# Moving the first four prompt-memory loads from SyncE's DMA queue to ScalarE's in a one-core decoder step

## The chip, the core and the metric

The kernel runs on one core of a Trainium2 chip. The core has TensorE (PE; its weight loads are listed apart as PEld), VectorE (DVE), ScalarE (ACT), GpSimd (POOL) and SyncE (SP). SP and ACT can each issue DMA transfers from their own instruction stream; the profile marks an issue as SPq or ACTq. The metric is the device time of one execution in microseconds.

## The reference

The program computes one layer of a decoder for 256 prompt tokens and 32 sample tokens together (T = 288 columns), in float32, with model width 2048. Cut to what matters here:

```
mk, mv = memory_kv(mem_prompt)          # rms_norm(mem) @ w_mem_kv, 256 memory tokens
h = rms_norm(x) * g_mix
proj = h @ w_in                         # conv, stick-breaking attention, memory query, gates
y_conv, y_sb, y_mem = three branches
x = x + (gates * branches summed) @ w_o
x = x + relu(rms_norm(x) @ w_up)^2 @ w_down
```

The first matrix product on the chip is the one for the prompt memory, `rms_norm(mem_prompt) @ w_mem_kv`: 256 memory tokens by 2048 features, into 512 value and 512 key columns. It is the only part that the change touches.

## The kernel before

All weights lie in DRAM as 504 slabs of 128 x 1024 float32 (512 KB), in the order in which they are used. A slab is loaded into a tile `wr`. Since TensorE is to give float32 accuracy, each slab is split: ScalarE rounds it to a high part `wh` (line 303), VectorE subtracts that from `wr` and leaves a low part `wl` (line 314). Activations are split the same way, and each product is three matmuls: high by high, low by high, high by low. There are four buffers of `wr` and four pairs of `wh` and `wl`.

The first 16 slabs hold the memory projection, two for each pair of feature blocks: one with value columns ("v"), one with key columns ("k"). These slabs are loaded in two halves of 256 KB. Beside them the raw prompt memory comes in eight tiles named `s` (128 x 512 float32), each in two halves of 128 KB (`memT`, line 394). A half is one feature block of 128 features by 256 memory tokens. For each half, ScalarE (line 345; for the very first half VectorE, line 341) multiplies by the gain and rounds to a high part `a`, VectorE makes the low part (line 361), and ScalarE squares the tile for the norm (lines 350 and 352).

On TensorE, `warm_up` runs seven matmuls on a constant tile (line 1419), then `mem_products` runs 32 turns of six 128x512 matmuls each (line 539). A turn takes one feature block and either the value or the key columns. The first four turns are (block 0, v), (block 0, k), (block 1, v), (block 1, k): they need both halves of the first two slabs and of the first `s` tile.

The order of instructions on every engine is fixed when the program is built. Each piece of work is a Python generator that asks for an engine, a time and the events it needs; a planner (`Order.run`) simulates the engines with fixed costs and emits the instructions in the order in which the simulation starts them. `add(gen, rank)` puts a generator in, and the lower rank goes first when two could start together. `loads` issues all loads on SP. `sp(...)` asks for 0.45 us of SP, and `order.landed(kb)` is the planner's guess of when a transfer lands.

Every DMA raises one of eight completion semaphores, `DMAHW0` to `DMAHW7`, taken in rotation over all DMAs of both queues in emission order. A DMA that takes a semaphore a second time first waits until its earlier user has landed; this wait stands in the instruction stream of the engine that issues the DMA.

Of the kernel before, what the change touches and what calls it, by code (L numbers as in the profile page):

```python
# [14 lines left out]
P = 128  # L15
# [59 lines left out]
class Order:  # L75
# [15 lines left out]
    def add(self, gen, rank, at=None):  # L91
        job = Job(gen, rank, self.now.ready if at is None and self.now else at or 0.0)
        self.jobs.append(job)
        was, self.now = self.now, job
        self.step(job)
        self.now = was
# [10 lines left out]
    def give(self, pool, n=1):  # L107
        self.pools[pool] += [self.now.ready] * n
# [45 lines left out]
def dve(n, *flags, **take):  # L154
    return Ask("DVE", 0.18 + n / 920.0, flags, **take)


def act(n, *flags, **take):
    return Ask("ACT", 0.22 + n / 1200.0, flags, **take)
# [10 lines left out]
def sp(*flags, **take):  # L170
    return Ask("SP", 0.45, flags, **take)
# [11 lines left out]
def tile_decoder_step(ctx: ExitStack, tc: tile.TileContext, xT, memT, wall, cvec, kmat, ptab,  # L183
                      kpool, vpool, mkc, mvc, hist,
                      yT, oK, oV, oCp, oCs, oMK, oMV):
    nc = tc.nc
# [15 lines left out]
    order = Order(bufs)  # L202
    give, add, done = order.give, order.add, order.set
# [3 lines left out]
    def tl(p, shape, dt=F32):  # L207
        cnt[0] += 1
        return pools[p].tile(shape, dt, tag=p, name=f"{p}_{cnt[0]}")
# [46 lines left out]
    def col(c):  # L256
        return cv[:, c:c + 1]
# [18 lines left out]
    def load_slab(s, part):  # L276
        sl = slabs[s]
        if part == 0:
            sl.raw = tl("wr", [P, SLAB])
        n = SLAB // sl.parts  # L280
        nc.sync.dma_start(sl.raw[:, part * n:(part + 1) * n], wall[s, :, part * n:(part + 1) * n])
        sl.landed[part].at = order.landed(n * P * 4 / 1e3)
# [5 lines left out]
    def due(s):  # L288
        return at_slab[1] + 2.9 * (s - at_slab[0])
# [3 lines left out]
    def cast_weights():  # L293
        todo = [(0, 0), (1, 0), (0, 1), (1, 1)] + [(s, i) for s in range(2, N_SLABS) for i in range(slabs[s].parts)]
        for s, i in todo:
            sl = slabs[s]
            n = SLAB // sl.parts
            cast_at[0] = s
            yield act(n, sl.landed[i], **({} if i else {"w": 1}))
            if i == 0:  # L300
                sl.h = shifted("wh", s)
            c = slice(i * n, (i + 1) * n)
            nc.scalar.copy(sl.h[:, c], sl.raw[:, c])  # L303
            sl.split[i].cast = order.now.ready
            add(sub_part(s, i), lambda s=s: 0 if due(s) - order.free["DVE"] < 5.0 else 4.5)
# [30 lines left out]
    def prep_mem(k2, raw, here):  # L336
        for i in range(2):
            if k2 + i == 0:
                yield dve(ML, here[i], a=2)
                a = hm[0] = Acts(ML)  # L340
                nc.vector.tensor_scalar_mul(a.h, raw[:, i], col(C_GMEM))
            else:
                yield act(ML, here[i], a=2)
                a = hm[2 * k2 + i] = Acts(ML)
                nc.scalar.mul(a.h, raw[:, i], col(C_GMEM + 2 * k2 + i))
            add(prep_low(a, raw[:, i], C_GMEM + 2 * k2 + i, ML, hm_in[2 * k2 + i]), 0.5 + 0.01 * k2)
        yield act(2 * ML, hm_in[2 * k2 + 1])
        if k2 == 0:
            mem_sum.append(tl("s", [P, 512]))
            nc.scalar.activation(mem_sum[0], raw.rearrange("p k t -> p (k t)"), AF.Square)  # L350
        else:
            nc.scalar.activation(raw, raw, AF.Square)
            yield dve(2 * ML)
            nc.vector.tensor_add(mem_sum[0], mem_sum[0], raw.rearrange("p k t -> p (k t)"))
            give("s")
            if k2 == KT // 2 - 1:
                done(sums_m)

    def prep_low(a, raw, c, n, flag):
        yield dve(n, late=Order.HOP)  # L360
        nc.vector.scalar_tensor_tensor(a.l, raw, col(c), a.h.bitcast(F32), op0=ALU.mult, op1=ALU.subtract)
        done(flag)

    def prep_x(k, raw, here, last):
        yield act(T, here, a=2)
        a = hx[k] = Acts()
        nc.scalar.mul(a.h, raw, col(C_GMIX + k))
        add(prep_low(a, raw, C_GMIX + k, T, hx_in[k]), 1.5 + 0.01 * k)
        yield act(T, hx_in[k], **({"t": 1} if k == 0 else {}))
        if k == 0:  # L370
            x_sum.append(tl("t", [P, T]))
            nc.scalar.activation(x_sum[0], raw, AF.Square)
        else:
            nc.scalar.activation(raw, raw, AF.Square)
            yield dve(T)
            nc.vector.tensor_add(x_sum[0], x_sum[0], raw)
        if last:
            give("k4")
        if k == KT - 1:
            done(sums_x)  # L380

    def loads():

        xs = [(0, 3), (3, 6), (6, 9), (9, 12), (12, 15), (15, 16)]
        for k2 in range(KT // 2):
            yield sp(s=1)
            raw = tl("s", [P, 512]).rearrange("p (k t) -> p k t", k=2)
            here = [Flag(), Flag()]
            for i in range(2):
                for what in ("vmk" if k2 + i == 0 else "mvk"):  # L390
                    if what == "m":
                        if k2 + i:
                            yield sp()
                        nc.sync.dma_start(raw[:, i], memT[:, 2 * k2 + i, :])
                        here[i].at = order.landed(131)
                        if i == 0:
                            add(prep_mem(k2, raw, here), 0.5 + 0.01 * k2)
                    else:
                        yield sp(**({} if i else {"wr": 1}))
                        load_slab(2 * k2 + "vk".index(what), i)  # L400
            if k2 >= 1 and xs:
                k0, k1 = xs.pop(0)
                yield sp(k4=1)
                x = tl("k4", [P, 1024])[:, :(k1 - k0) * T].rearrange("p (k t) -> p k t", k=k1 - k0)
                nc.sync.dma_start(x, xT[:, k0:k1, :])
                there = Flag()
                there.at = order.landed(147 * (k1 - k0))
                for k in range(k0, k1):
                    add(prep_x(k, x[:, k - k0], there, k == k1 - 1), 1.5 + 0.01 * k)
            if k2 == 1:  # L410
                yield sp()
                nc.sync.dma_start(cv[:, C_BGATE:], cvec[:, C_BGATE:])
            if k2 == 2:
                yield sp()
                nc.sync.dma_start(km, kmat)
                km_in.at = order.landed(213)
                yield sp()
                nc.sync.dma_start(pt, ptab)
                pt_in.at = order.landed(1) + 20.0
        for s in range(KT, N_SLABS):  # L420
            yield sp(wr=1)
            load_slab(s, 0)
# [39 lines left out]
    def mem_norm():  # L462
        yield dve(ML, sums_m)
        both = mem_sum[0][:, :ML]
        nc.vector.tensor_add(both, both, mem_sum[0][:, ML:])
        yield act(ML, t=2)
        h, l = tl("t", [P, T], F32R)[:, :ML], tl("t", [P, T], F32R)[:, :ML]
        nc.scalar.copy(h, both)
        yield dve(ML)
        nc.vector.tensor_sub(l, both, h.bitcast(F32))  # L470
        give("s")
        yield pe(0.45, pa=1)
        ss = bank("pa")[:, :2 * MT].rearrange("p (m c) -> p m c", c=2)
        for m in range(MT):
            for x in (h, l):
                nc.tensor.matmul(ss[:, m], x[:, m * P:(m + 1) * P], ones_r[:, 0:2], start=x is h, stop=x is l)
        give("t", 2)
        ss = ss[:, :, 0]
        yield from rsqrt_of(ss, MT, D_MODEL, nm[0][:, :MT], nm[1][:, :MT], rm)
        give("pa")  # L480
        done(rm_done)
# [510 lines left out]
    def read_pages():  # L992

        for i in range(2 * NB):
            yield Ask("SP", 0.6, (pt_in,), 2.5)
            pages.append(nc.sync.value_load(pt[0:1, i:i + 1], min_val=0, max_val=kpool.shape[0] - 1))
        done(pages_in)
# [457 lines left out]
                yield from main_tile(u, down_tile(j, c == D_FF // D_MODEL - 1))  # L1455

    with tc.manual_schedule():
        add(loads(), 1.0)
        add(cast_weights(), lambda: 0 if due(cast_at[0]) - order.free["ACT"] < 6.0 else 4.5)
        add(mem_norm(), 0.6)  # L1460
        add(sum_norm(x_sum, D_MODEL, rx, rx_done, sums_x), 0.6)
        add(main(), 20.0)
        add(conv_norm(), 8.0)
        add(read_pages(), 4.0)
        add(make_homes(), 1.0)
        order.run()
# [156 lines left out]
```

## Time and profile before

| what | value |
|---|---|
| median of three runs | 1629.76 us (1629.35 to 1629.9) |
| the profiled execution, its own time | 1629.18 us |
| span of the profiled execution, first to last instruction | 1627.2 us |
| PE busy, share of the span | 1622.6 us, 100% |
| DVE, ACT, POOL busy | 994.0, 736.9, 139.0 us |
| bytes moved by DMA | 305.33 MB, mean 188 GB/s |
| granted TensorE clock, mean | 1.000 |

The span starts with the first instruction; the time of the execution is 1.98 us longer than the span. Times in the timeline count from the start of the span. Matmuls are pipelined, so the duration of a matmul row is longer than the distance from one matmul to the next; distances are read from the starts. In the timeline a row with "x2" is two like instructions merged, with the start of the first and the stretch of both.

### The profile page before, as it was taken

The numbers are of one execution on the slowest core, as the hardware profiler recorded it, in microseconds if no ns is written. First come the engines' busy times: TensorE is split into PE (matmuls) and PEld (weight loads), VectorE is DVE, ScalarE is ACT, GpSimd is POOL, SyncE is SP. The second block draws the span as 40 slices with busy tenths as digits, with TensorE's granted clock in tenths as the row PEclk, the third lists the DMA queues.
The fourth block names the chain that finished last, engine by engine and source line by source line (L and its number), as shares of the span: only waits on it lengthen the run. The fifth ranks groups of instructions, "written<-read, shape, count | busy, mean of one in ns | idle before, by whom it ended". The sixth has DMA issues, their size and how long they took to land.

```text
span 1627.2 us, 30882 instructions
## 1 busy us (share of the span) xinstructions
PE 1622.6 (100%) x12744; PEld 1606.7 (99%) x12744; DVE 994.0 (61%) x1478; ACT 736.9 (45%) x1082; POOL 139.0 (9%) x106
## 2 busy tenths in 40 slices
PE   9999999999999999999999999999999999999999
PEld 7999999999999999999999999999999999999999
DVE  8899888877777655565555544455445554455543
ACT  8746766654434534444443333333333333333332
POOL 0020000000000000001222200121001210022100
PEclk9999999999999999999999999999999999999999
DMA  9787476677755555556655555555555555555663
GB/s 336 217 176 263 141 270 198 208 260 265 243 167 171 170 170 172 166 164 206 194 173 169 170 171 168 169 169 169 168 168 169 169 169 168 170 169 169 180 192 101
DMA packets 107103, 305.33 MB, mean 188 GB/s; under 512 B 19922, under 2 KB 29522, under 8 KB 106962
## 3 DMA queue, kind: packets, MB, share of 16 engines
q1 hardware_dynamic: 106818, 303.33, 60.1%
q8 instruction: 100, 1.64, 0.4%
q14 instruction: 41, 0.34, 0.1%
q10 hardware_dynamic: 144, 0.02, 0.0%
HBM read 296.99 MB, written 6.32 MB: 186 GB/s over the span
## 4 chain that ended last, share of the span: by engine, by line
PE 100%; POOL 0%; DVE 0%; issue 0%; POOLq 0%
PE pm L486 93%; PE pm L539 3%; PE pa L486 1%; PE pl L1021 1%; PE pl L1195 0%; PE pa L860 0%; PE pa L862 0%; PE pa L861 0%; PE pl L1035 0%; PE pa L1419 0%; PE pa L1157 0%; PE pa L825 0%; PE pa L915 0%; PE pa L1171 0%; PE pa L1129 0%; PE pa L1112 0%
## 5 line engine op out<-in xcount | busy, mean ns | idle before, releaser
L303 ACT CAST wh<-wr 128x1024 fp32r<-128x1024 f32 (+1 forms) x520 | 530.4, 1023 | 638.3 <-PE pm L486 581.8
L486 PE MATMUL pm<-a,wh 128*128 128x288 f32 x5184 | 737.1, 293 | 0.0
L314 DVE TENSOR_TENSOR wl<-wr,wh 128x1024 fp32r<-128x1024 f32 (+1 forms) x520 | 620.1, 1196 | 190.7 <-ACT wh L303 188.5
L486 PEld LDWEIGHTS pm<-a,wh 128*128 128x128 f32 x5184 | 696.2, 188 | 0.0
L486 PE MATMUL pm<-a,wl 128*128 128x288 f32 x2592 | 399.2, 293 | 0.0
L486 PEld LDWEIGHTS pm<-a,wl 128*128 128x128 f32 x2592 | 359.0, 188 | 0.6 <-issue 0.6
L486 PE MATMUL pm<-k,wh 128*128 128x288 f32 x2400 | 337.8, 292 | 0.0
L486 PEld LDWEIGHTS pm<-k,wh 128*128 128x128 f32 x2400 | 321.5, 188 | 0.0
L486 PE MATMUL pm<-k,wl 128*128 128x288 f32 x1200 | 181.8, 292 | 0.0
L486 PEld LDWEIGHTS pm<-k,wl 128*128 128x128 f32 x1200 | 165.5, 188 | 0.0
L1356 POOL TENSOR_TENSOR t<-t 128x288 f32<-128x288 f32 x64 | 96.7, 1511 | 599.5 <-DVE t L1353 599.5
L1370 DVE TENSOR_TENSOR a<-a,pm 128x288 f32<-128x288 f32 x64 | 29.1, 455 | 122.3 <-PE pm L486 122.3
L1353 DVE SCALAR_TENSOR_TENSOR t<-pm,rx 128x288 f32<-128x288 f32 x64 | 29.3, 458 | 90.2 <-PE pm L486 90.2
L1359 ACT CAST k<-t 128x288 fp32r<-128x288 f32 x60 | 25.9, 433 | 124.1 <-POOL t L1356 124.1
L1272 DVE TENSOR_TENSOR t<-pm,rx 128x288 f32<-128x288 f32 x48 | 22.0, 458 | 70.9 <-PE pm L486 70.9
L1361 DVE TENSOR_TENSOR k<-t,k 128x288 fp32r<-128x288 f32 x60 | 27.4, 459 | 59.3 <-ACT k L1359 59.3
L717 DVE SCALAR_TENSOR_TENSOR a<-a,cv,a 128x256 f32<-128x256 f32 x120 | 59.5, 496 | 1.3
L1342 POOL TENSOR_TENSOR t<-t,t 128x288 f32<-128x288 f32 x15 | 21.2, 1415 | 418.0 <-ACT t L1339 418.0
L539 PE MATMUL pm<-wh,a 128*128 128x512 f32 x128 | 35.0, 395 | 0.0
L486 PE MATMUL pm<-s,wh 128*128 128x288 f32 x160 | 33.7, 292 | 0.0
L539 PEld LDWEIGHTS pm<-wh,a 128*128 128x128 f32 x128 | 24.2, 190 | 5.9 <-ACT wh L303 1.0
L486 PEld LDWEIGHTS pm<-s,wh 128*128 128x128 f32 x160 | 25.6, 188 | 0.0
(211 smaller groups left out, 744.3 us busy)
## 6 DMA issues: line engine op xcount, KB each, us to landing
wr<-in_wall SPq DMA_DIRECT2D x488, 512.0 KB, 3.7
wr<-in_wall SPq DMA_DIRECT2D x32, 256.0 KB, 4.8
k<-in_kpool SPq DMA_DIRECT2D x32, 256.0 KB, 5.8
k<-in_vpool SPq DMA_DIRECT2D x32, 256.0 KB, 6.2
k<-in_mkc SPq DMA_DIRECT2D x8, 512.0 KB, 9.0
k<-in_mvc SPq DMA_DIRECT2D x8, 512.0 KB, 7.3
t<-in_xT SPq DMA_DIRECT2D x16, 144.0 KB, 3.8
out_yT<-a SPq DMA_DIRECT2D x16, 144.0 KB, 1.9
```

The costliest lines, as they stand in the source:

```text
L303: nc.scalar.copy(sl.h[:, c], sl.raw[:, c])
L314: nc.vector.tensor_sub(sl.l[:, c], sl.raw[:, c], sl.h[:, c].bitcast(F32))
L486: nc.tensor.matmul(ps, w, a, start=(first and i == 0), stop=(last and i == len(todo) - 1))
L539: nc.tensor.matmul(ps[m], y[:, m * P:(m + 1) * P], z[:, w], start=(k == 0 and j < 2), stop=(k == KT - 1 and j in (4, 5)))
L717: nc.vector.scalar_tensor_tensor(c[:, :NP], up[:, k:k + NP], w, c[:, :NP], op0=ALU.mult, op1=ALU.add)
L1272: nc.vector.tensor_mul(g, ps, rx)
L1342: nc.gpsimd.tensor_add(sq_sum[0], sq_sum[0], res[0])
L1353: nc.vector.scalar_tensor_tensor(r, ps, 0.0, r2, op0=ALU.max, op1=ALU.mult)
L1356: nc.gpsimd.tensor_mul(r, r, r)
L1359: nc.scalar.copy(a.h, r)
L1361: nc.vector.tensor_sub(a.l, r, a.h.bitcast(F32))
L1370: nc.vector.tensor_add(x1[j], x1[j], ps)
```

## The change

A new generator `lead` issues both halves of the first two `s` tiles (four transfers of 128 KB) from ScalarE's instruction stream. `loads` then leaves the memory out for the first two pairs of feature blocks and issues only the weight halves there, in the order v, k, v, k. Everything after that is issued on SP as before.

```diff
+    LEAD = 2
+
+    def lead():
+
+        for k2 in range(LEAD):
+            for i in range(2):
+                yield Ask("ACT", 0.45, **({} if i else {"s": 1}))
+                if i == 0:
+                    raw = tl("s", [P, 512]).rearrange("p (k t) -> p k t", k=2)
+                    here = [Flag(), Flag()]
+                    add(prep_mem(k2, raw, here), 0.5 + 0.01 * k2)
+                nc.scalar.dma_start(raw[:, i], memT[:, 2 * k2 + i, :])
+                here[i].at = order.landed(131)
+
     def loads():
...
         for k2 in range(KT // 2):
-            yield sp(s=1)
-            raw = tl("s", [P, 512]).rearrange("p (k t) -> p k t", k=2)
-            here = [Flag(), Flag()]
+            if k2 >= LEAD:
+                yield sp(s=1)
+                raw = tl("s", [P, 512]).rearrange("p (k t) -> p k t", k=2)
+                here = [Flag(), Flag()]
             for i in range(2):
-                for what in ("vmk" if k2 + i == 0 else "mvk"):
+                for what in ("vk" if k2 < LEAD else "mvk"):
                     if what == "m":
-                        if k2 + i:
-                            yield sp()
+                        yield sp()
                         nc.sync.dma_start(raw[:, i], memT[:, 2 * k2 + i, :])
...
     with tc.manual_schedule():
+        add(lead(), 0.0)
         add(loads(), 1.0)
```

Since the planner sees other times, it numbers the tiles otherwise and changes the order in a few places later in the program too.

On SP, at the start of the program, the order before was as follows. `wr_126` is the first value slab, `wr_129` the first key slab, `wr_136` and `wr_140` the next pair; `s_117` and `s_134` are the first two memory tiles. A row names the semaphore that the issue waits for.

```order
L281 DMA wr_126<-in_wall 128x512
L394 DMA s_117<-in_memT 128x256
L281 DMA wr_129<-in_wall 128x512
L394 DMA s_117<-in_memT 128x256
L281 DMA wr_126<-in_wall 128x512
L281 DMA wr_129<-in_wall 128x512
L394 DMA s_134<-in_memT 128x256
L281 DMA wr_136<-in_wall 128x512 [waits DMAHW0_49]
L281 DMA wr_140<-in_wall 128x512 [waits DMAHW1_49]
L394 DMA s_134<-in_memT 128x256 [waits DMAHW2_49]
```

On SP with the change, the same place (`wr_119` is now the first value slab, `wr_130` the first key slab, `wr_137` and `wr_139` the next pair):

```order
L281 DMA wr_119<-in_wall 128x512
L281 DMA wr_130<-in_wall 128x512
L281 DMA wr_119<-in_wall 128x512
L281 DMA wr_130<-in_wall 128x512
L281 DMA wr_137<-in_wall 128x512 [waits DMAHW0_49]
L281 DMA wr_139<-in_wall 128x512 [waits DMAHW2_49]
L281 DMA wr_137<-in_wall 128x512 [waits DMAHW3_49]
L281 DMA wr_139<-in_wall 128x512 [waits DMAHW4_49]
```

The four memory transfers are gone from SP: the first half of the key slab stands second instead of third, and the eight weight halves follow each other.

On ACT, at the start of the program, before (`wh_138` and `wh_153` are the high parts of the first value and key slab; `cv` is a table of gains):

```order
L228 ACT_TABLE_LOAD
L240 DMA cv<-in_cvec 128x48
L303 CAST wh_138<-wr_126 128x512 [waits DMAHW0_49]
L303 CAST wh_153<-wr_129 128x512 [waits DMAHW3_49]
L345 ACTIVATE a_157<-s_117,cv 128x256 [waits DMAHW4_49,DMAHW2_49]
L303 CAST wh_138<-wr_126 128x512 [waits DMAHW5_49]
L303 CAST wh_153<-wr_129 128x512 [waits DMAHW6_49]
```

On ACT with the change (`wh_149` and `wh_163` are now those high parts, `s_132` is the second memory tile; "x2" is two like rows in a row):

```order
L228 ACT_TABLE_LOAD
L240 DMA cv<-in_cvec 128x48
L393 DMA s_117<-in_memT 128x256 x2
L393 DMA s_132<-in_memT 128x256
L393 DMA s_132<-in_memT 128x256 [waits DMAHW1_49]
L303 CAST wh_149<-wr_119 128x512 [waits DMAHW0_49]
L345 ACTIVATE a_157<-s_117,cv 128x256 [waits DMAHW5_49,DMAHW2_49]
L303 CAST wh_163<-wr_130 128x512
L345 ACTIVATE a_166<-s_132,cv 128x256 [waits DMAHW7_49]
L303 CAST wh_149<-wr_119 128x512 [waits DMAHW3_49]
```

All four memory issues now stand ahead of ScalarE's first cast, and the last of them is the ninth DMA of the program, so it waits for a semaphore, `DMAHW1`. Who raises that semaphore is told by VectorE's rows with the change, where the subtraction that reads the first half of the key slab `wr_130` waits for it:

```order
L361 SCALAR_TENSOR_TENSOR a_143<-s_117,cv,a_142 128x256 [waits DVE_49]
L314 TENSOR_TENSOR wl_160<-wr_119,wh_149 128x512 [waits DMAHW0_49,Activation_49]
L361 SCALAR_TENSOR_TENSOR a_158<-s_117,cv,a_157 128x256 [waits DMAHW5_49,Activation_49]
L314 TENSOR_TENSOR wl_169<-wr_130,wh_163 128x512 [waits DMAHW1_49,Activation_49]
L361 SCALAR_TENSOR_TENSOR a_167<-s_132,cv,a_166 128x256 [waits DMAHW7_49,Activation_49]
```

What moved: the cast of the first key half had a wait of its own before; now it has none, because an instruction further up on its engine, the issue of the second half of `s_132`, has waited for the same transfer.

## The prediction

> **What bounds the kernel now.** I read the page first, for the bound, then the waits of the weight loads, then a table by stage, then the timeline of the first 12 us, where the change lies.
>
> ```profile
> span 1627.2 us, 30882 instructions
> PE 1622.6 (100%) x12744; PEld 1606.7 (99%) x12744; DVE 994.0 (61%) x1478; ACT 736.9 (45%) x1082; POOL 139.0 (9%) x106
> ...
> PE 100%; POOL 0%; DVE 0%; issue 0%; POOLq 0%
> ```
>
> The chain that ended last (the third line) is TensorE's own work from end to end. So only two things can move the time: TensorE's amount of work, which the change leaves as it is, and idle or slow stretches on TensorE. The waits of the weight loads, in order of their total (us in total, times, longest), show how few there are:
>
> ```profile
> PEld pa L1419 <- POOL eps L233: 1.3, 1, 1.3
> PEld pm L539 <- ACT wh L303: 1.0, 2, 0.6
> PEld pm L486 <- issue: 0.6, 2, 0.4
> PEld pm L539 <- DVE wl L314: 0.4, 1, 0.4
> ```
>
> The first is the start of the program. The second and fourth are in the memory stage: 1.4 us in which TensorE's loads waited for a split weight. All other waits together are small. The table by stage (stretch, its length, then busy time and count of PE, PEld, DVE, ACT, POOL, the clock, the DMA share, GB/s):
>
> ```profile
> 0.00:10.00 10.00, 8.68 (x25) 6.05 (x26) 4.40 (x9) 5.63 (x10) 1.24 (x8) 1.00 0.78 248
> 10.00:50.00 40.00, 40.00 (x180) 33.22 (x179) 37.50 (x68) 36.61 (x75) 0.25 (x2) 1.00 0.98 333
> 50.00:540.00 490.00, 490.00 (x4207) 483.73 (x4206) 399.73 (x731) 273.13 (x501) 19.59 (x17) 1.00 0.68 214
> ```
>
> Only the first 10 us have room. From 10 us on PE is busy all the time, though between 10 and 50 us ACT and DVE are over 90% busy and the DMA engines 98%. Now the first 12 us, cut to the rows that matter (start, length, engine, line, what):
>
> ```profile
> 0.75 0.40 SPq L281 DMA_DIRECT2D wr<-in_wall  x1
> 0.77 0.40 ACTq L240 DMA_DIRECT2D cv<-in_cvec  x1
> 1.21 0.42 SPq L394 DMA_DIRECT2D s<-in_memT  x1
> ...
> 1.32 3.35 PE L1419 MATMUL pa<-wh 128*128 128x512 f32 x7 [1.32 <-POOL eps L233]
> 1.67 0.44 SPq L281 DMA_DIRECT2D wr<-in_wall  x1
> ...
> 3.76 0.62 ACT L303 CAST wh<-wr 128x512 fp32r<-128x512 f32 x1 [1.74 <-DMA wr<-in_wall]
> ...
> 4.11 0.35 DVE L341 TENSOR_SCALAR a<-s,cv 128x256 fp32r<-128x256 f32 x1 [2.17 <-DMA s<-in_memT]
> 4.41 0.69 DVE L314 TENSOR_TENSOR wl<-wr,wh 128x512 fp32r<-128x512 f32 x1
> ...
> 4.61 1.19 PE L539 MATMUL pm<-wh,a 128*128 128x512 f32 x2
> ...
> 5.18 0.76 PEld L539 LDWEIGHTS pm<-wl,a 128*128 128x128 f32 x2
> 5.60 0.90 PE L539 MATMUL pm<-wl,a 128*128 128x512 f32 x2
> ...
> 6.21 0.80 SPq L281 DMA_DIRECT2D wr<-in_wall  x2
> 6.21 0.62 ACT L303 CAST wh<-wr 128x512 fp32r<-128x512 f32 x1 [1.84 <-DMA wr<-in_wall]
> ...
> 6.34 1.28 PE L539 MATMUL pm<-wh,a 128*128 128x512 f32 x4
> ...
> 8.19 1.53 PE L539 MATMUL pm<-wh,a 128*128 128x512 f32 x6
> ...
> 9.33 0.41 PEld L539 LDWEIGHTS pm<-wl,a 128*128 128x128 f32 x2
> 9.46 0.98 ACT L345 ACTIVATE a<-s,cv 128x256 fp32r<-128x256 f32 x2
> 9.56 0.62 PE L539 MATMUL pm<-wl,a 128*128 128x512 f32 x2
> ...
> 10.01 1.07 PE L539 MATMUL pm<-wh,a 128*128 128x512 f32 x4
> ...
> 10.60 1.66 ACT L303 CAST wh<-wr 128x512 fp32r<-128x512 f32 x3 [0.15 <-DMA wr<-in_wall]
> ...
> 11.37 1.07 PE L539 MATMUL pm<-wh,a 128*128 128x512 f32 x4
> ```
>
> The first cast starts at 3.76, when the first value half has landed; the first real matmul follows at 4.61. The second cast, of the first key half (issued third, at 1.67), waits until 6.21; SP's issue at 6.21 waits for the same transfer. So that half took 6.21 - 1.67 = 4.54 us.
>
> I measure TensorE's start by one number. At full rate a turn of six matmuls takes 11.37 - 10.01 = 1.36 us, 0.227 each, and from 8.19 on the starts keep that step (8.19 + 6 x 0.227 = 9.55, the next row). At 8.19 ten matmuls are done; had they run at full rate without waits, the first would have started at 8.19 - 2.27 = 5.92. This **even start** of 5.92, against the real 4.61, holds all that is lost at the beginning: 1.3 us. Part of that is slow matmuls: the seven of the warm-up took 3.35 us, 0.48 each, and the first two real ones stand (5.60 - 4.61)/2 = 0.50 apart, a small wait included. After that the chain has 192 matmuls in one piece, to 49.61, followed by PE alone:
>
> ```profile
> 4.67 44.94 PE pm L539 x192
> ```
>
> So the end of the program moves by what the even start moves. This bounds the gain too: even with no wait and no slow matmul, the even start can't come before 4.61 with the first cast where it is, so at most 1.3 us can be won. About 0.2% is what a measurement of this kernel can tell from no change, 3.26 us.
>
> **The change part by part.** SP loses four issues of 0.42 to 0.43 us. Its first weight half stays where it is, at 0.75; the first key half goes from 1.67 to about 1.2, the others from 2.63 and 3.1 to 1.7 and 2.1. The ninth DMA and those after it wait for a free semaphore, before and after, so SP stands still from about 2.5 until the first value half has landed (3.76): of the 1.7 us that SP wins, little comes through.
>
> ACT gains four issues of about 0.40 us each (the row at 0.77). Three of them, from 1.17 to about 2.4, cost nothing: ACT waited 1.74 us there for the first weight. The first memory half is issued at 1.2 as before, so VectorE's first product (4.11) isn't later by itself. The fourth issue is the costly one. It waits for the first key half, and it stands ahead of the first cast. So the first cast, which before waited for the first value half alone, now also waits for the first key half, and then for 0.40 us of issue. Behind it queue all of ACT's casts, behind these DVE's subtractions, and behind both TensorE.
>
> How late is that? Call L the landing of the first key half. No row shows two loaded queues at once, so I bound it by the durations of weight halves in the first 20 us, from issue to landing:
>
> ```profile
> DMA to landing us min/median/max: 3.0/4.7/5.3
> ```
>
> Issued at 1.2, it lands between 4.2 and 6.5; by its own 4.54 at 5.75, by the median at 5.9. I take 5.8. The 3.0 belongs to the very first transfer, which had the DMA engines to itself, so it is the far end. The bytes say the same: before, 664 KB of issued data (256 + 128 + 24 + 256) had to move until this half was in; now 512 KB of weights, 24 KB of gains and whatever of the other queue's memory halves comes between, up to 256 KB, so 536 to 792 KB. The transfer rate in half microseconds (last column, GB/s) shows why it took so long:
>
> ```profile
> 3.00:3.50 0.50, 0.50 (x2) 0.40 (x2) 0.00 (x0) 0.00 (x0) 0.00 (x0) 1.00 1.04 340
> ...
> 4.00:4.50 0.50, 0.50 (x2) 0.00 (x0) 0.39 (x2) 0.38 (x1) 0.00 (x0) 1.00 0.60 107
> 4.50:5.00 0.50, 0.50 (x2) 0.42 (x2) 0.50 (x1) 0.00 (x0) 0.00 (x0) 1.00 0.76 121
> ...
> 5.50:6.00 0.50, 0.50 (x2) 0.34 (x2) 0.00 (x0) 0.00 (x0) 0.00 (x0) 1.00 1.01 344
> ```
>
> Between 4 and 5 us the engines moved a third of what they move before and after, with transfers outstanding. Nothing in the profile names the reason. If it comes again L is near 5.8; if not, about 1 us earlier.
>
> The Trainium skill has a rule that speaks against the change: "DMA: Bandwidth & Descriptors", section "Issuing engines are not separate DMA queues", says that transfers of all issuing engines run on the same 16 DMA engines and interleave, so that a second issuer saves only issue time. By it the key half gains at most the 0.46 us of its earlier issue (L = 5.75, 1631.2 us); were the second queue free of the first, L would be 4.2 and the time 1629.7. The trace agrees as far as it goes: 340 GB/s from one queue is already the rate of the full stage (333).
>
> From L to the even start: the fourth issue takes 0.40 and a handover of about 0.05, so the first cast starts at L + 0.45. In the trace the load of the low part starts 5.18 - 3.76 = 1.42 after the cast; at full rate its matmul follows 9.56 - 9.33 = 0.23 later, as the third of its turn. The even start is therefore 1.42 + 0.23 - 2 x 0.227 = 1.20 after the cast: L + 1.65 = 7.45. Against 5.92 that is **1.53 us later**; with L of 4.2 it is 0.07 earlier, with 6.5 it is 2.23 later.
>
> What is late next? After the delay ACT has everything at hand and its casts follow each other by about 0.53 us (three in 1.66), its products by 0.47 (two in 0.98). Its tenth piece, the second half of the third slab, then starts at 6.25 + 4.5 = 10.75, where it stood at 10.60 before: ACT has caught up, because it no longer waits for the second cast. The transfers it needs there were issued by 5.9 and need at most 5.3 us, while TensorE wants them from 7.45 + 5 x 1.36 = 14.2 on. So no second wait follows, and TensorE, itself 1.5 us later, has more cover than before in the stage where ACT and DVE are over 90% busy. The planner's later reordering costs nothing: the same matmuls in another order, on an engine that never waits there.
>
> The rows hold one more unknown, the slow matmuls. At the start each costs 0.20 to 0.25 us extra; from 6.34 on four take 1.28. TensorE will now be idle from 4.67 to about 7.1. If the slowness is over by then, nothing is added (the number above is at full rate). If TensorE has to earn it again, a slow matmul costs 0.43 - 0.227 = 0.2. (A full-rate row of four lasts 1.07 where its four steps are 0.91, so the last one's drain adds 0.16; with twice that the seven of the warm-up give (3.35 - 0.32)/7 = 0.43.)
>
> **The rivals.** *Early landing.* The rate hole doesn't come again or the second queue lets the weight pass: L of 4.5, even start 6.15, 0.23 us later: 1630.0 us. For it speaks the earlier issue as second transfer, against it the memory halves that now run beside it instead of behind.
>
> *The slow clock comes back.* Slow matmuls ran from 1.32 to about 6.2, 4.9 us. If the idle gap makes TensorE start over, it is slow from 7.1 to 12.0. In 4.9 us it does 11.4 matmuls at 0.43 instead of 21.6, so it loses 10.2 x 0.227 = 2.3 us; with the 1.53 that is 3.8, or 1633.6: slower. It decides from a loss of 3.26 - 1.53 = 1.73 us on, nine slow matmuls, slow until about 10.9. Against it: TensorE's gap is shorter than its warm-up was.
>
> The Trainium skill, "TensorE: Matmul & The Clock Gate", Part 1, describes this as a half-rate clock that is lifted after a busy window of about 3.4 us and comes back after an idle one. An estimate by that page is a loss of up to 3.4 x (1 - 0.227/0.43) = 1.6 us, 1632.9 in all. The rows of slow and fast matmuls agree with the two rates; no row here shows what a gap of 2.4 us does.
>
> *The casts aren't held.* ACT's waiting issue doesn't stop what is behind it, and all early halves land sooner: the first cast stays at 3.76 and the even start goes to 4.96, 0.96 us earlier, 1628.8 us. Against it speaks ACT's order, in which the waiting issue stands ahead of the cast.
>
> **How the numbers follow.** The profiled execution took 1629.18 us, 0.58 under the median of 1629.76; the shift is added to the median: 1629.76 + 1.53 = 1631.3. Its own range, with L from 5.2 to 6.5 and a few slow matmuls, is 1630.7 to 1632.6. Chances: this case 0.60, early landing 0.20, the slow clock 0.14, the gain 0.04, something elsewhere in the program 0.02. The range runs from early landing with the runs' scatter of 0.3 us, 1629.6, to just under the slow clock's decision, 1633.0. Slower by over 0.2% are the slow clock and half of the last case, 0.15; faster by over 0.2% needs 3.26 us where 1.3 can be had, 0.01; the rest is the same, 0.84.
>
> **What would show it.** Right: in the changed kernel's timeline ACT's fourth memory issue at about 5.8, its first cast at about 6.3 right behind, the first real matmul at about 7.1, and no wait for a second cast. Wrong: a first cast before 5 (early landing, or a wait that holds nothing), matmuls 0.43 apart after 8 us (the clock), or any new wait of TensorE after 10 us.

## The result and the profile after

The changed kernel takes 1631.43 us (median of 22 runs, 1630.42 to 1632.74), the kernel before 1629.55 us on the same chips (22 runs, 1628.91 to 1630.08). The ratio is 1.0013, its 95% interval 1.0007 to 1.0018: 1.88 us more, inside the 0.2% that was called the same, but to the slow side. The runs spread twice as wide as before. The profiled execution took 1632.72 us and is one of the slowest; a second trace of the same kernel, taken in an experiment below, took 1631.21.

The chain of waits of the first trace, cut to its start (start, length, what; rows of 0.07 us and less between these are left out), shows what the beginning now hangs on:

```profile
0.75 0.40 SPq L281
1.21 4.42 DMA wr<-in_wall
5.64 0.33 ACTq L393
6.02 0.63 ACT wh L303
6.69 46.68 PE pm L553 x192
```

Before, the chain was PE's own work from 1.32 on. It now goes from SP's issue through the transfer of the first key half (landed 1.21 + 4.42 = 5.63) to ScalarE's fourth memory issue, its first cast and the first real matmul. The 192 matmuls of the memory stage end at 53.37, where they ended at 49.61; the span is 3.7 us longer. What was lost at the start is still lost at the end.

TensorE's timeline in the first trace, and below it in the second:

```profile
1.32 3.35 PE L1433 MATMUL pa<-wh 128*128 128x512 f32 x7 [1.32 <-POOL eps L233]
6.69 1.22 PE L553 MATMUL pm<-wh,a 128*128 128x512 f32 x2 [2.02 <-ACT wh L303]
7.71 1.05 PE L553 MATMUL pm<-wl,a 128*128 128x512 f32 x2
8.57 1.91 PE L553 MATMUL pm<-wh,a 128*128 128x512 f32 x4
10.27 1.05 PE L553 MATMUL pm<-wl,a 128*128 128x512 f32 x2
11.13 2.32 PE L553 MATMUL pm<-wh,a 128*128 128x512 f32 x6
13.28 0.39 PE L553 MATMUL pm<-wl,a 128*128 128x512 f32 x1
```

```profile
6.15 1.22 PE L553 MATMUL pm<-wh,a 128*128 128x512 f32 x2 [1.47 <-ACT wh L303]
7.16 1.06 PE L553 MATMUL pm<-wl,a 128*128 128x512 f32 x2
8.02 1.77 PE L553 MATMUL pm<-wh,a 128*128 128x512 f32 x4
9.64 0.62 PE L553 MATMUL pm<-wl,a 128*128 128x512 f32 x2
10.09 1.54 PE L553 MATMUL pm<-wh,a 128*128 128x512 f32 x6
11.47 0.62 PE L553 MATMUL pm<-wl,a 128*128 128x512 f32 x2
```

The row at 13.28 is the 17th real matmul, so the even start is 13.28 - 16 x 0.227 = 9.65; in the second trace it is 11.47 - 3.63 = 7.84 (before: 5.92). In the first trace the matmuls stay 0.43 apart until past 12 us: a pair lasts 1.05 and not 0.62. In the second they are fast from 9.6 on. The first real matmuls of the two executions are 0.54 us apart, and the slow matmuls make it 1.8 us at the even start.

VectorE's first product, in the first and in the second trace:

```profile
5.91 0.35 DVE L341 TENSOR_SCALAR a<-s,cv 128x256 fp32r<-128x256 f32 x1 [3.97 <-DMA s<-in_memT]
```

```profile
5.47 0.35 DVE L341 TENSOR_SCALAR a<-s,cv 128x256 fp32r<-128x256 f32 x1 [3.53 <-DMA s<-in_memT]
```

It stood at 4.11 before. The first memory half is issued at 1.20, as before, and yet comes 1.4 to 1.8 us later.

### The profile page after: what moved, and what is told of

It reads as the page before. It is cut to its first block, busy times and chain, and to the rows that moved or that the text cites. A ratio compares the mean times of both kernels' runs of the same rounds, so it can differ in the third digit from the quotient of the medians.

```text
span 1630.9 us, 30883 instructions
## 1 busy us (share of the span) xinstructions
PE 1624.4 (100%) x12744; PEld 1608.3 (99%) x12744; DVE 993.9 (61%) x1478; ACT 738.6 (45%) x1082; POOL 139.2 (9%) x106
## 4 chain that ended last, share of the span: by engine, by line
PE 99%; DMA 0%; ACT 0%; DVE 0%; SPq 0%; ACTq 0%; issue 0%
PE pm L500 93%; PE pm L553 3%; PE pa L500 1%; PE pl L1035 1%; PE pl L1209 0%; DMA wr<-in_wall 0%; PE pa L876 0%; PE pa L874 0%; PE pa L875 0%; PE pl L1049 0%; PE pa L839 0%; PE pa L1171 0%; PE pa L1143 0%; PE pa L929 0%; PE pa L1185 0%; PE pa L1126 0%
```

## The experiments

Medians are of 11 runs beside runs of the kernel before on the same chip; the level of the kernel before differs by up to 0.4 us between the chips, so each time is given over that of before. The intervals of the ratios are about 0.0009 wide to each side, which is 1.5 us. So by its interval a loss of about 1.0 to 1.6 us is not clear of none; that it is one rests on the runs beside it, since there nearly every run is above every run of the kernel before. Differences of some tenths between two variants are not told apart. Times of instructions come from one trace each.

**Three halves on ScalarE, none that waits.** The second half of the second tile goes back to SP. The code was rewritten for this around a list of what ScalarE issues; the edit is shown by that list, and the first line stands for the changed kernel.

```diff
-LEADS = [(0,0), (0,1), (1,0), (1,1)]   # (tile, half) issued by ScalarE
+LEADS = [(0,0), (0,1), (1,0)]          # the rest by SP, in the order of before
```

> As the changed kernel, but the second half of the second memory tile goes back to SP, so ScalarE issues three memory halves and none of its issues waits. Theory 'hold' (the waiting issue ahead of the first cast is the cause): the first cast starts near 3.8 us again instead of 6.02, the first real matmul near 4.7, and the time is that of before or less, 1628.8 to 1629.7 us. Theory 'late tile' (the first memory half itself lands late on ScalarE's queue, at 5.8 in the changed kernel's trace against 4.1 before, and would hold TensorE by itself): the first cast starts near 3.8, but VectorE's first product stays at about 5.9 and the first matmul at about 6.3, so the time falls by 0.3 to 0.8 at most, to 1630.5 to 1631.2 us.

Measured: 1631.12 us, 1.86 over before. ScalarE's timeline, and VectorE's first product:

```profile
3.70 0.62 ACT L303 CAST wh<-wr 128x512 fp32r<-128x512 f32 x1 [1.68 <-DMA wr<-in_wall]
7.41 0.51 ACT L345 ACTIVATE a<-s,cv 128x256 fp32r<-128x256 f32 x1 [3.10 <-DMA s<-in_memT]
7.83 0.60 ACT L303 CAST wh<-wr 128x512 fp32r<-128x512 f32 x1
```

```profile
5.49 0.35 DVE L341 TENSOR_SCALAR a<-s,cv 128x256 fp32r<-128x256 f32 x1 [3.55 <-DMA s<-in_memT]
```

The cast is back at 3.70, and it helps nothing: the first real matmul (5.99) waits for the product at 5.49. In ScalarE's order the product of the second memory half stands ahead of the second cast and holds it until 7.8. So without the hold the loss is as large as with it, and the late tile is enough for it. The time lies at the upper end of what "late tile" gave; the loss is above it, since the kernel before is faster on this chip. What makes it so large are slow matmuls: TensorE is not idle again, and the 17th real matmul comes 5.89 us after the first, where 16 steps at full rate take 3.63.

```profile
5.99 1.19 PE L555 MATMUL pm<-wh,a 128*128 128x512 f32 x2 [1.32 <-DVE a L341]
```

**Two halves on ScalarE.** Here the first memory half stays second on SP.

```diff
-LEADS = [(0,0), (0,1), (1,0), (1,1)]
+LEADS = [(0,1), (1,0)]
```

> As the changed kernel, but ScalarE issues only the second half of the first memory tile and the first half of the second; the first half of the first tile stands second on SP as before, the second half of the second tile goes to SP too. No issue of ScalarE waits. Theory 'late tile': VectorE's first product is back at about 4.1 us and the first matmul at 4.6 to 4.7; the key half, third on SP with two memory halves beside it instead of ahead, lands at 5.5 to 6.2; time 1628.8 to 1629.6 us, some 2 us under the changed kernel. Theory 'hold': the same time as with three halves on ScalarE. If sharing the engines with any second queue delays the weights, the key half lands after 6.2 and the time is 1629.6 to 1630.5 us.

Measured: 1631.70 us, 2.44 over before. All three forecasts missed. The first matmul is early, at 4.98, but then TensorE runs dry:

```profile
4.98 1.19 PE L555 MATMUL pm<-wh,a 128*128 128x512 f32 x2 [0.31 <-DVE a L341]
5.97 1.05 PE L555 MATMUL pm<-wl,a 128*128 128x512 f32 x2
6.82 0.70 PE L555 MATMUL pm<-wh,a 128*128 128x512 f32 x2
8.77 0.50 PE L555 MATMUL pm<-wh,a 128*128 128x512 f32 x1 [1.25 <-ACT wh L303]
```

ScalarE's products of both halves that it loads stand ahead of its second cast and wait until 7.30. The planner assumes that a transfer lands by its place in one common row; these halves on ScalarE's queue landed later than that, and the order it writes is then wrong.

**A longer warm-up on the changed kernel.**

```diff
-        for i in range(7):
+        for i in range(12):
             nc.tensor.matmul(junk, warm[:, :P], warm[:, :512], start=True, stop=True)
```

> The changed kernel with 12 instead of 7 matmuls in the warm-up, nothing else moved; at 0.43 us each they end at about 6.5 us, just before the first real matmul at 6.7. Theory 'clock' (the idle stretch from 4.7 to 6.7 makes the matmuls slow again, which cost 2.4 us in the profiled execution and an amount that varies between runs): the real matmuls are 0.23 apart from the start, the even start is at 7.2 and the time 1630.5 to 1631.0 us, with a spread as narrow as before's (1.2 us instead of 2.3). Rival (the late start alone makes the difference and the slow matmuls hide in waits): 1631.4 us as now, with the same spread.

Measured: 1630.26 us, 1.00 over before, 1629.68 to 1630.47. The loss falls from 1.88 to 1.00 and the spread from 2.3 to 0.8 us. The time is a little under what "clock" expected, the narrow spread is as it said.

```profile
1.32 4.99 PE L1433 MATMUL pa<-wh 128*128 128x512 f32 x12 [1.32 <-POOL eps L233]
6.32 0.74 PE L553 MATMUL pm<-wh,a 128*128 128x512 f32 x2
7.09 0.74 PE L553 MATMUL pm<-wl,a 128*128 128x512 f32 x2
7.67 1.08 PE L553 MATMUL pm<-wh,a 128*128 128x512 f32 x4
...
10.53 0.62 PE L553 MATMUL pm<-wl,a 128*128 128x512 f32 x2
```

Four real matmuls take 1.08 from the third pair on, against 1.91 in the first trace above. The row at 10.53 is the 17th real matmul, so the even start is 10.53 - 3.63 = 6.90, 0.98 later than before. Five useless matmuls more make the program 0.9 us shorter.

**A shorter warm-up on the kernel before.** The same line with 3; no transfer is touched.

> The kernel before with 3 instead of 7 matmuls in the warm-up, nothing else moved, so TensorE is idle from about 2.7 to 4.6 us, as long as in the changed kernel, while no transfer is touched. Theory 'clock': matmuls stay 0.43 apart beyond 6.2 us, up to 12 us in some runs; each costs 0.2 us, so 1630.0 to 1632.0 us and a spread of about 2 us. Rival (the idle stretch is harmless): 1629.6 us, spread 1.2 us.

Measured: 1630.30 us, 1.04 over before; spread 1.05 us (1629.53 to 1630.58), narrower than expected. The idle stretch from 3.0 to 4.45 costs about a microsecond:

```profile
1.32 1.65 PE L1419 MATMUL pa<-wh 128*128 128x512 f32 x3 [1.32 <-POOL eps L233]
4.45 1.19 PE L539 MATMUL pm<-wh,a 128*128 128x512 f32 x2 [1.49 <-DVE a L341]
5.45 1.05 PE L539 MATMUL pm<-wl,a 128*128 128x512 f32 x2
6.30 2.04 PE L539 MATMUL pm<-wh,a 128*128 128x512 f32 x4
8.14 1.01 PE L539 MATMUL pm<-wl,a 128*128 128x512 f32 x2
8.98 1.32 PE L539 MATMUL pm<-wh,a 128*128 128x512 f32 x5
```

**The changed kernel again.**

> The changed kernel as it is, on the chip of these runs, to compare with. 1.5 to 2.2 us over before, spread over 2 us. Its trace: ScalarE's fourth issue ends at 5.3 to 6.1 us; if the clock theory holds, the last matmul spaced 0.43 lies at another time than in the first trace (12.4 us), anywhere from 6.7 to 13, and the time of the profiled execution moves with it by 0.2 us for each slow matmul.

Measured: 1631.24 us, 2.09 over before, 1629.86 to 1631.76. Its trace is the second one above. ScalarE's fourth issue starts at 5.10 and its first cast at 5.47; then the product of the second memory half waits 1.50 us more:

```profile
5.10 0.33 ACTq L393 DMA_DIRECT2D s<-in_memT  x1
5.47 0.62 ACT L303 CAST wh<-wr 128x512 fp32r<-128x512 f32 x1 [3.45 <-DMA wr<-in_wall]
7.59 0.51 ACT L345 ACTIVATE a<-s,cv 128x256 fp32r<-128x256 f32 x1 [1.50 <-DMA s<-in_memT]
```

**Whole tiles on ScalarE.** Two transfers of 256 KB in rows of 2 KB instead of four of 128 KB in rows of 1 KB. The planner is told that they land later, so that they don't get ahead of the casts.

```diff
-                nc.scalar.dma_start(raw[:, i], memT[:, 2 * k2 + i, :])
-                here[i].at = order.landed(131)
+            nc.scalar.dma_start(raw, memT[:, 2 * k2:2 * k2 + 2, :])
+            here[0].at = order.landed(262) + 2.2 * k2
+            here[1].at = here[0].at + 1.3
```

> As the changed kernel, but ScalarE issues each of the two memory tiles as one transfer of 256 KB with rows of 2 KB, instead of two of 128 KB with rows of 1 KB; the same bytes on the same queue. With two issues fewer, none of ScalarE's waits. Theory 'packets' (the 16 engines take packets of the two queues in turn, one row a packet, so rows of 1 KB against SP's 2 KB leave ScalarE's queue a third of the bytes, 0.10 of 0.30 MB per us in the changed kernel): the queue now gets about half, 0.14 to 0.16 MB per us between 4 and 5 us, the whole first tile lands at 5.3 to 5.9 us (its halves: 5.8 and 7.0 in the changed kernel), the key half a little later, at 5.5 to 6.1; first real matmul at 6.1 to 6.6, time 1 to 1.8 us over before. Rival (the engines serve SP's queue first, whatever the rows): still a third, the tile lands at 7.0 or later, first matmul after 7.8, time over 2.5 us over before.

Measured: 1632.46 us, 3.31 over before. The queues' rows for 4 to 6 us (packets, MB, share of 16 engines; q1 is SP's queue, q10 ScalarE's), of the changed kernel's first trace and of this one:

```profile
q1 hardware_dynamic: 215, 0.38, 68.2%
q10 hardware_dynamic: 232, 0.21, 33.0%
```

```profile
q10 hardware_dynamic: 148, 0.27, 52.3%
q1 hardware_dynamic: 149, 0.27, 40.6%
```

Both queues get about as many packets, whatever a packet holds: with 1 KB against 2 KB ScalarE's has a third of the bytes, with 2 KB on both it has half. That is what "packets" says, and it speaks against a fixed preference for SP's queue. The whole tile is there at 6.3 (VectorE's first product at 6.29), where the second of its halves came at 7.1 and 7.6 in the changed kernel's two traces. The times failed: the tile is later than the 5.9 that "packets" allowed, with a lower rate in this stretch (0.54 against 0.59 MB), and the slow matmuls come on top. The time alone lies in the rival's range; the bytes, the tile and the first matmul (6.79) don't fit the rival. The Trainium skill, "DMA: Bandwidth & Descriptors", section "Queues, rings and completion order", describes this: each engine takes its queues in turn, a packet at a time. The rows above agree.

**Whole tiles and a longer warm-up.** The kernel above with 12 warm-up matmuls.

> The kernel with two whole memory tiles on ScalarE, with 12 instead of 7 warm-up matmuls. Theories 'packets' and 'clock' together: first real matmul at 6.2 to 6.6, no slow matmul after it, 0.2 to 0.9 us over before with a spread near 1 us. If it is under before, moving the tiles can pay once the clock and the rows are seen to.

Measured: 1630.99 us, 1.84 over before (1630.74 to 1633.3), twice what was expected at most, and with a wide spread. The longer warm-up won 1.47 us here. What is left goes with the late tile: VectorE's first product stands at 6.36, the first real matmul 0.50 behind it, at 6.86. So half of the bytes isn't enough.

```profile
6.36 0.35 DVE L341 TENSOR_SCALAR a<-s,cv 128x256 fp32r<-128x256 f32 x1 [4.41 <-DMA s<-in_memT]
```

**Three halves and a longer warm-up.** The first experiment's kernel with 12 warm-up matmuls.

> The kernel with three memory halves on ScalarE and none that waits, with 12 instead of 7 warm-up matmuls. It has neither the held cast nor the idle stretch; what is left over before is the late memory tile alone. Theory 'late tile': first real matmul at 6.0 to 6.5 us behind VectorE's product at 5.5 to 5.9, and 0.4 to 1.0 us over before, about level with the changed kernel with 12 warm-up matmuls (1.0 over). Theory 'hold': without the hold, level with before or under it.

Measured: 1630.22 us, 1.07 over before (1629.6 to 1631.28), level with the changed kernel with the long warm-up (1.00) and a little above what "late tile" said. So taking the hold of the first cast away wins nothing once the tile is late. It does not leave the late tile alone, though. In this trace, which is of the slowest run, the second cast still stands behind the product of the second memory half, and TensorE waits for it:

```profile
7.73 0.51 ACT L345 ACTIVATE a<-s,cv 128x256 fp32r<-128x256 f32 x1 [3.31 <-DMA s<-in_memT]
8.14 0.60 ACT L303 CAST wh<-wr 128x512 fp32r<-128x512 f32 x1
```

TensorE is idle for 0.69 us there, until 8.80. Besides, the warm-up itself ran until 6.4, and the first real matmul follows it directly, at 6.45, though its operands were there some 0.5 us earlier.

**The hold alone.** ScalarE's first two casts change places in the kernel before; no transfer is moved.

```diff
-        todo = [(0, 0), (1, 0), (0, 1), (1, 1)] + ...
+        todo = [(1, 0), (0, 0), (0, 1), (1, 1)] + ...
```

> The hold alone: the kernel before with ScalarE's first two casts in the other order, so that the cast of the value half queues behind that of the key half, which waits for its landing at about 6.2 us; no transfer is moved, the memory tile is there at 4.1 us. The prediction's step (the hold costs its full length when it stands on the path): the value cast starts at 6.7 to 6.9 instead of 3.7, the first real matmul at 7.5 to 7.8, the even start at 7.9 to 8.1 without slow matmuls; 2.0 to 2.2 us over before, and with slow matmuls after the idle stretch of 3 us up to 4.5. If the hold costs little by itself, as the equal times of the two kernels with the long warm-up, with and without it, could also be read, it is under 1 us over before.

Measured: 1632.94 us, 3.74 over before, within what the prediction's step gives with slow matmuls. The three casts in a row start when the key half is there, the value half's as the second of them:

```profile
6.05 1.66 ACT L303 CAST wh<-wr 128x512 fp32r<-128x512 f32 x3 [4.02 <-DMA wr<-in_wall]
```

The memory tile is in time here (first product at 4.16), and the first real matmul still starts at 7.24 instead of 4.61. So a wait ahead of the first cast reaches TensorE in its full length when nothing else is late. How much of the 3.74 is slow matmuls was not measured: the value half's cast starts at about 6.58 (6.05 and one step of 0.53), which puts the even start at 7.78 without them, 1.86 later, as an estimate. In the changed kernel two waits, for the key half and for the memory tile, end within half a microsecond of each other, and taking the first away uncovers the other.

**Is the dip from the 1 KB rows?** In the kernel before, one pair of SP's issues swapped (value half ahead of the second memory half).

```diff
-                for what in ("vmk" if k2 + i == 0 else "mvk"):
+                for what in ("vmk" if k2 == 0 else "mvk"):
```

> The kernel before with one pair of issues on SP swapped: the second half of the first value slab goes ahead of the second half of the first memory tile. All loads stay on SP. It asks whether the dip of the transfer rate between 4 and 5 us, which holds up the key half until 6.2, comes from the 1 KB rows of the memory half right behind it. If so the key half lands at 5.2 to 5.8, the even start comes 0.3 to 0.8 us earlier, and the time is 0.3 to 0.8 us under before. Rival (the dip comes with the moment and not with the rows): the key half lands at 6.0 to 6.4 again and the time is within 0.2 us of before.

Measured: 1629.34 us against 1629.20, no difference. The dip came again, 157 GB/s, and the second cast started at 6.62, later than either forecast:

```profile
6.62 1.30 ACT L303 CAST wh<-wr 128x512 fp32r<-128x512 f32 x2 [2.21 <-DMA wr<-in_wall]
```

So it is not the rows of that half.

**The other way round.** All memory on SP as before, the first key half alone on ScalarE (the edit in short).

```diff
+    def lead():
+        yield Ask("ACT", 0.45, wr=1)
+        load_slab(1, 0, nc.scalar)      # issues on nc.scalar; loads() leaves it out
```

> The other way round: all memory halves stay on SP as before, and ScalarE issues only the first key half, 256 KB in rows of 2 KB, right after the gains; no issue of ScalarE waits. Theory 'packets': against SP's 1 KB memory rows the 2 KB rows get two thirds of the bytes, so the key half lands at 4.6 to 5.3 us instead of 6.2 and the second cast starts then; the first memory half, second on SP, pays for it and lands at 4.5 to 5.3 instead of 4.1, so the first real matmul starts at 5.2 to 6.0. If the gain at the second cast outweighs, the time is up to 0.7 us under before; if the later first matmul does, up to 0.6 us over. A loaded second queue should also lift the transfer rate between 4 and 5 us from 100 to 160 GB/s to over 220.

Measured: 1630.74 us, 1.57 over before, above what was expected either way. The key half came only 0.5 us earlier (second cast at 5.74) and the first memory half 1.5 us later (first product at 5.60), both later than "packets" gave:

```profile
5.60 0.35 DVE L341 TENSOR_SCALAR a<-s,cv 128x256 fp32r<-128x256 f32 x1 [3.66 <-DMA s<-in_memT]
5.74 0.62 ACT L303 CAST wh<-wr 128x512 fp32r<-128x512 f32 x1 [1.39 <-DMA wr<-in_wall]
```

What one queue wins the other loses. The first matmul needs the memory half, the second turn the key half.

## Why the prediction held, and which of its steps did not

**The bound** was right: in both traces of the changed kernel the even start moved by 3.73 and 1.92 us and the executions by 3.54 and 2.03. In the ten other traces it moved by 0.45 to 4.00, and the execution with it to within 0.25 us, but for the kernel with two halves (1.89 against 2.36). By the spans (3.7 and 2.2 us longer) everything after the first 14 us cost at most 0.3 us, the planner's new order included. The prediction had put this at nothing, and it is one wait of TensorE for a product of ScalarE at about 56.7 us in the second trace, which the trace of the kernel before does not have; where it comes from stays open:

```profile
PEld pm L500 <- ACT a L603: 0.3, 1, 0.3
```

That SP's freed issue time brings nothing was not tried by itself; no kernel here came out clearly under before.

**The hold** was right in place and size. The key half landed at 5.63 and, judged by ScalarE's fourth issue, at about 5.1 in the second trace, against 5.8 with the dip of the transfer rate between 4 and 5 us and 4.8 without; the cast followed 0.39 and 0.37 later, against 0.45. So the half landed 0.6 and 1.1 us ahead of the kernel before (6.21), more than the 0.46 us by which the half is issued earlier.

**"The first memory half isn't later by itself"** was wrong. It came at 5.91 and 5.47. ScalarE's queue gets packets in turn but half-size ones, so a third of the bytes, while SP's weights take the rest; the whole tiles in larger rows bear this out in bytes, though they were no faster on the whole. The step put the transfer on a queue of its own and forgot what it shares. The sum survived by luck: the hold ended within 0.11 us of this lateness in both traces and covered it.

**"ACT has everything at hand"** was wrong too: the second memory half came late for the same reason, and ScalarE waited 0.5 and 1.5 us for it with its casts queued behind. TensorE felt little of it: its loads waited 0.3 us for the second cast in the second trace and not at all in the first.

**The two terms of the sum.** The start was put at 1.53 us. With the slow matmuls taken away by the longer warm-up, 1.00 is left in the median and 0.98 at the even start of its trace. The term was half again too large: the dip did not come (277 to 304 GB/s between 4 and 5 us in the three traces with this order of loads), and the first cast started at 5.47 to 6.02 instead of 6.25. The slow matmuls were put at 0 in the likeliest case. They are worth 1.88 - 1.00 = 0.88 us in the median and 9.65 - (6.02 + 1.20) = 2.43 in the first trace, just what the rival "the slow clock comes back" gave (2.3); in the second trace 7.84 - (5.47 + 1.20) = 1.17, small waits included. So that rival and the forecast were not alternatives; both happened in both traces, in different parts. The total of 1631.3 came out close to 1631.43 with one term too large and one missing, and that is luck.

**"Comes back"** is not what the rows show. The seven warm-up matmuls of the changed kernel are all slow in both traces (3.35 us), so nothing was fast yet when the gap began at 4.67; the gap put off the end of the slowness. That it is TensorE's clock is inferred from the step of 0.43 us and from the runs with other warm-ups: the profile's column of the granted clock says 1.00 in these stretches too.

**The Trainium skill's clock rule** ("TensorE: Matmul & The Clock Gate", Part 1) wants a busy window of about 3.4 us, on a window that runs freely. The runs agree: the same program is slow until past 12 us in one trace and until 9.5 in the other, and an idle stretch of 1.5 us within the warm-up (3.0 to 4.45) already costs 1.0 us. Twelve warm-up matmuls, started at 1.32 in three traces, took 4.41, 4.99 and 5.30 us, so the slowness ended at another time in each with nothing idle between.

## What to carry to other kernels

A second DMA queue is no second lane: engines take packets of the loaded queues in turn, so count bytes and row sizes of everything that is in flight. Larger rows give a queue a larger share, but no kernel here that moved a transfer to the second queue came out faster. An issue that waits stands in the stream of its engine; look what is queued behind it, and what else would be late if it were gone. Where TensorE starts, a gap of 1.5 us cost 1.0 us here though no transfer was touched, so let the warm-up reach to the first real matmul.

## What the runs showed of the hardware

The dip between 4 and 5 us goes with the single queue. Windows of 4 to 5 us (last column GB/s), of the swapped pair and of the hold alone, both with all early loads but the small table on SP:

```profile
4.00:5.00 1.00, 1.00 (x3) 0.38 (x2) 0.84 (x2) 0.41 (x1) 0.00 (x0) 1.00 0.92 157
```

```profile
4.00:5.00 1.00, 0.68 (x2) 0.00 (x0) 0.81 (x2) 0.00 (x0) 0.00 (x0) 1.00 0.71 100
```

and of the changed kernel (second trace) and of the kernel with the key half on ScalarE:

```profile
4.00:5.00 1.00, 0.67 (x2) 0.00 (x0) 0.00 (x0) 0.00 (x0) 0.00 (x0) 1.00 0.88 277
```

```profile
4.00:5.00 1.00, 0.68 (x2) 0.00 (x0) 0.00 (x0) 0.36 (x1) 0.00 (x0) 1.00 1.04 264
```

The four traces with one loaded queue show 100 to 157 GB/s here, the nine with two show 219 to 326. So at this moment more was moved with a second loaded queue. The Trainium skill ("DMA: Bandwidth & Descriptors", section "Issuing engines are not separate DMA queues") grants a second issuer only the time of issuing; these rows show more than that. Why the single queue stalls there stays open; the one guess that was tried, the 1 KB rows of the memory half behind the key half, is out. The extra bytes did not help: the even start is not ahead of 5.92 in any trace.
